# A hybrid S5 and attention layer on one core: TensorE's order fixed from the first load, the context's products one channel tile behind, k as filler work, and the modulation sums in free columns of the drives' banks

## The chip, the cores and the metric

The kernel runs on one core of a Trainium2 chip. The metric is the device time of one execution in microseconds (us); smaller is better. The core has five engines with a queue of their own each: PE (TensorE, matrix products into PSUM banks, with the loading of weights shown as PEld), DVE (VectorE), ACT (ScalarE), POOL (GpSimd), and SP (SyncE), which here only issues DMA transfers.

## What is computed

One layer over 512 latent tokens and a prefix of 256 context tokens, 1024 channels wide, all in float32. Cut to what this case is about:

```python
mod   = silu(c) @ w_mod + b_mod            # six vectors of 1024 for the latents
mod_c = silu(c_ctx) @ w_mod + b_mod        # for the context only two of them are used
sh1, sc1, g1, sh2, sc2, g2 = split(mod, 6)
h  = rmsnorm(x, norm1_w) * (1 + sc1) + sh1
hc = rmsnorm(ctx, norm1_w) * (1 + csc1) + csh1
q, k, v, u, g = split(h @ w_in)            # 1024, 256, 256, 512, 2048 columns
kc, vc, uc = split(hc @ w_in[:, Q_END:U_END])
q, k, kc = rope(rmsnorm(q)), rope(rmsnorm(k)), rmsnorm(kc)
attn  = softmax(q @ [kc, k].T / sqrt(128)) @ [vc, v]
y_ssm = s5_bidirectional(u, uc, ...)       # complex-diagonal scans, both directions
x = x + g1 * merge(attn, y_ssm, g)         # gates, glu, output projection
x = x + g2 * conv_ffn(rmsnorm(x) * (1 + sc2) + sh2)
out = rmsnorm(x) * final_norm_w
```

## The kernel before

**Tiles.** Channels lie on partitions: x is eight tiles of 128x512, ctx eight of 128x256. Every large product is made of three products of rounded parts (`mm3`, L122): hi by hi, hi by lo, lo by hi. A weight tile is loaded in pieces of 128x512 into a ring `wr` of three buffers; ACT rounds it (`wh`, L135) and POOL takes the rest (`wl`, L136). All loads are issued by SP, one after the other, each when its buffer is free.

**PSUM.** Eight banks: two of tag "a" (mod, kp, kss, vp, proj, mods), two of tag "b" (n, uc, gps, kps, yt), and two pairs of tag "s" (`bank2`; ul, then gp).

**Stages on PE, in order.** (1) The sums of squares of x (L357 and L358: eight products with ones, one for each tile's squares) and of ctx (L339, L341: added on DVE first). (2) For each channel tile k: `mod_sums(k)`, 16 rows of work on the first two modulation vectors; a copy of the sum to SBUF (L390); `mod_turn(k)`, which turns it onto partitions (L383); the scale and shift (L400, L402); h and c in two parts (L416 to L418); and the products of u, latent (`ul`) and context (`uc`), with the weight tile `wu`. (3) u is copied to SBUF, written to DRAM (`ud`) and read back in another layout (`u`, `s5_u`). (4) The keys (`kp`, their norms `kss`). (5) S5 in four blocks s of two halves h each: `s5_build` (tables W and H on DVE), `s5_lags` (kps, then the trip `ldr`, `tp` through DRAM), `s5_drive` (transposes gps, then the drive products gp), `s5_half` (products, scans and products back on DVE), `s5_out` (the readout, into the columns 384 to 511 of the drive's two banks) and `s5_end` (`yt`). (6) Attention, merging and the feed-forward network.

**What sets the order.** Up to the first drive the framework's scheduler orders all queues; from `pinned[0] = True`, just ahead of `s5_drive(0, 0)`, PE runs in program order (`pe`, L120). From there `filler()` supplies steps of v (`vp`) and gate products (`proj`), and `weave` puts them between the steps of the S5 chain. Between the filler's own steps, one step of `mods_all` (L738) is put in for every two and a half: it works out the other four modulation vectors, 16 pieces of 256 columns. Each piece is two visits of four matmuls (`mods<-wm`, L743) into a bank of tag "a" of its own, a copy of the row on ACT (L749), and a visit that turns it (`mods<-cst,vr`, L383) with two ACT operations (L755) that take the result. Its weights `wm` are 32 loads of 512 KB into two buffers.

Of the kernel before, what the change touches and what calls it, by code (L numbers as in the profile page):

```python
# [29 lines left out]
LOADS = "xxwcw"  # L30
WU_V = ()
PO2 = 2
GAP, F0, F1, F2, F3, WM = 2, 8, 13, 5, 2, 2
# [29 lines left out]
def hybrid_layer_kernel(ctx: ExitStack, tc: tile.TileContext, io, out):  # L63
    nc = tc.nc
    V, A, G, T, S = nc.vector, nc.scalar, nc.gpsimd, nc.tensor, nc.sync
# [54 lines left out]
    def pe(ins):  # L120

        if pinned[0]:  # L122
            nosync(ins, last[0])
        last[0] = ins
# [67 lines left out]
    x = [None] * 8  # L192
    cx = k8("y8", [KT, LC])
    i = 0
    for what in LOADS:
        if what == "x":
            xt = k8("x8", [4, L])
            S.dma_start(xt, io["x"][:, 4 * i:4 * i + 4])
            x[4 * i:4 * i + 4] = [xt[:, j] for j in range(4)]
            i += 1  # L200
        elif what == "c":
            S.dma_start(cx, io["ctx"])
            S.dma_start(sd, io["sd"])
        else:
            load_wm()
# [23 lines left out]
    behind = [None]  # L229

    def tt(o, a, b, op, eng=V):
        i = eng.tensor_tensor(o, a, b, op=op).ins  # L232
        if behind[0] is not None:
            nosync(i, behind[0])
# [17 lines left out]
    z1, z2, ang8 = sm("n"), sm("n2"), sm("a8")  # L252
    r1, r8 = sm("r1"), sm("r8")
    wrap(ang, r1, z1)
    V.tensor_scalar(r1, r1, PI_LO, -PI_LO, op0=OP.min, op1=OP.max)
    table("silu_and_others")
    sn, co, ab = sm("sn"), sm("co"), sm("ab")
    act(sn, r1, AF.Sin)
    A.activation(ab, r1, AF.Abs)
    act(co, ab, AF.Sin, scale=-1.0, bias=half_pi)  # L260
    V.tensor_scalar(ang8, ang, float(TC), None, op0=OP.mult)
    wrap(ang8, r8, z2)
    fr, fhi, flo = sm("fr"), sm("fhi"), sm("flo")
    V.tensor_scalar(fr, r8, 1.0 / TWO_PI, None, op0=OP.mult)
    V.tensor_scalar(fhi, fr, 192.0, None, op0=OP.add)
    V.tensor_scalar(fhi, fhi, 192.0, None, op0=OP.subtract)
    tt(flo, fr, fhi, OP.subtract)

    pw = tz([8, 2, 32], "tab", 2)
    pf = tz([8, 2, 32], "tab", 2)  # L270
    tt(pw[:, 0, 0], mag, co, OP.mult)
    tt(pw[:, 0, 1], mag, sn, OP.mult)

    def cmul(o, a, b, n):
# [41 lines left out]
    for kk, w, n in ((ka, wa, 6), (kb, wb, 16)):  # L316
        def by_s(t):
            return t.rearrange("p (s c) a -> p s (c a)", s=4)
# [127 lines left out]
    def run(gen):  # L446
        for _ in gen:
            pass
# [736 lines left out]
```

## Time and profile before

| | us |
|---|---|
| three timed executions | 983.08, 982.51, 981.89 (median 982.51) |
| the profiled execution | 982.85 |
| its span, first to last instruction | 980.8 |
| PE busy | 927.6 (95%) |
| DVE, ACT, POOL busy | 485.7, 417.0, 364.8 |

The profiled execution is 0.34 us above the median, and 2.05 us of it lie outside the span. PE is the engine that is nearly always busy. Its granted clock is shown as PEclk, 1.00 for the full 2.4 GHz and 0.5 for 1.2 GHz. A matmul's record is its own duration; how far apart two starts are says what a row of work costs PE, since they overlap. Matmuls in plain float32 (n, mod, mods, gp, kps, gps, yt) show two records for each one that the program writes, transposes one.

The rows shown further on divide the span by what PE does: to the first u product, to the last one, to the end of the first readout, to the first norm of a query (from where on attention begins), and the rest.

### The profile page before, as it was taken

To read this page: it belongs to the slowest core of one execution; us is meant where nothing else is said; L and a number is where in the kernel's file an instruction comes from. 1 tells how busy PE (TensorE), PEld (TensorE's weight loads), DVE (VectorE), ACT (ScalarE), POOL (GpSimd) and SP (SyncE) were. 2 spreads that over 40 slices of the span, in tenths; PEclk is the share of its full clock that TensorE was granted. 3 is DMA by queue.
4 is the path that set the end of the run, shared out by engine and by line. 5 is a ranking of instruction groups with operands and counts; after the bars stand their busy time and mean duration, and the time that the engine had idled before them with its cause. 6 is when DMAs were issued, how large, how long until landed. Compare 5 with 4: busy or idle time off the path is not lost.

```text
span 980.8 us, 15658 instructions
## 1 busy us (share of the span) xinstructions
PE 927.6 (95%) x6142; PEld 736.8 (75%) x6142; DVE 485.7 (50%) x935; ACT 417.0 (43%) x795; POOL 364.8 (37%) x282
## 2 busy tenths in 40 slices
PE   5998889898999999999999999999999999999996
PEld 2676766565667778888778899888888888888886
DVE  7557788484507677777524464333333333200103
ACT  7325544333228445445433443443434444432332
POOL 1214131224124122222235520555565565554553
PEclk9989999899999999999999999999999999999999
DMA  9516546464532111111114620323323233333332
GB/s 363 231 44 194 160 135 189 130 191 155 152 128 76 33 44 48 53 52 44 43 57 138 193 87 1 108 86 99 96 88 104 88 97 98 83 103 94 96 108 86
DMA packets 56378, 107.24 MB, mean 109 GB/s; under 512 B 6001, under 2 KB 19057, under 8 KB 54641
## 3 DMA queue, kind: packets, MB, share of 16 engines
q1 hardware_dynamic: 56304, 106.25, 34.4%
q8 instruction: 48, 0.79, 0.3%
q14 instruction: 26, 0.20, 0.1%
HBM read 101.02 MB, written 5.21 MB: 108 GB/s over the span
## 4 chain that ended last, share of the span: by engine, by line
PE 67%; DVE 8%; ACT 5%; issue 5%; DMA 2%; POOL 1%; DVEq 0%; ACTq 0%; POOLq 0%
PE up L127 25%; PE down L127 12%; PE proj L127 10%; PE po L127 6%; PE glu L127 3%; PE sc L127 3%; PE pab L127 3%; PE tps L906 2%; DMA wr<-wo 2%; ACT P L108 1%; ACT wh L135 1%; DVE w L232 1%; DVE p L232 1%; DVE p L587 1%; DVE k L232 1%
## 5 line engine op out<-in xcount | busy, mean ns | idle before, releaser
L136 POOL TENSOR_TENSOR wl<-wr,wh 128x512 fp32r<-128x512 f32 x226 | 312.0, 1401 | 574.7 <-ACT wh L135 565.9
L127 PE MATMUL up<-t,wh 128*128 128x512 f32 (+1 forms) x768 | 226.5, 379 | 1.3 <-DVE t L1023 0.7
L135 ACT CAST wh<-wr 128x512 fp32r<-128x512 f32 x226 | 128.1, 610 | 132.6 <-PE down L127 40.5
L127 PEld LDWEIGHTS up<-t,wh 128*128 128x128 f32 x768 | 141.1, 190 | 31.2 <-DVE t L1023 1.5
L127 PE MATMUL proj<-h,wh 128*128 128x512 f32 x384 | 145.3, 425 | 7.0 <-ACT x L108 4.0
L127 PE MATMUL up<-t,wl 128*128 128x512 f32 (+1 forms) x384 | 145.3, 378 | 0.0
L127 PEld LDWEIGHTS proj<-h,wh 128*128 128x128 f32 x384 | 74.4, 194 | 35.4 <-issue 11.7
L127 PEld LDWEIGHTS up<-t,wl 128*128 128x128 f32 x384 | 73.0, 190 | 14.5
L127 PE MATMUL proj<-h,wl 128*128 128x512 f32 x192 | 77.2, 402 | 0.8 <-POOL wl L136 0.8
L1057 DVE SCALAR_TENSOR_TENSOR zc<-up,pv,zc 128x511 f32<-128x511 f32 x44 | 33.0, 750 | 88.6 <-ACT zc L1056 88.6
L1056 ACT ACTIVATE zc<-up,pv 128x512 f32<-128x512 f32 x44 | 34.2, 778 | 74.8 <-PE up L127 74.8
L1088 DVE SCALAR_TENSOR_TENSOR x<-down,mods,x 128x512 f32<-128x512 f32 (+1 forms) x9 | 6.2, 691 | 91.5 <-PE down L127 91.5
L135 ACT CAST pth<-tps 128x512 fp32r<-128x512 f32 x48 | 28.1, 586 | 47.3 <-PE tps L906 47.3
L127 PE MATMUL glu<-w,wh 128*128 128x512 f32 x128 | 42.5, 393 | 0.0
L127 PEld LDWEIGHTS proj<-h,wl 128*128 128x128 f32 x192 | 37.5, 195 | 6.0 <-POOL wl L136 1.1
L894 DVE TENSOR_REDUCE sc<-sc 128x1 f32<-128x768 f32 x32 | 30.7, 959 | 20.1 <-PE sc L127 20.1
L136 DVE TENSOR_TENSOR ptl<-tps,pth 128x512 fp32r<-128x512 f32 x48 | 33.0, 687 | 13.3 <-ACT pth L135 13.0
L127 PE MATMUL sc<-g,qh 128*128 128x256 f32 (+1 forms) x128 | 36.8, 341 | 0.0
L127 PE MATMUL down<-h,wh 128*128 128x512 f32 x112 | 35.6, 389 | 0.0
L108 ACT ACTIVATE P<-sc,nb,rq 128x768 f32<-128x768 f32 x32 | 31.9, 996 | 5.0 <-DVE nb L895 4.0
L127 PE MATMUL po<-pth,g 128*128 128x512 f32 x96 | 33.0, 424 | 1.0 <-ACT pth L135 0.6
L1058 DVE SCALAR_TENSOR_TENSOR zc<-up,pv,zc 128x511 f32<-128x511 f32 x44 | 33.0, 750 | 1.6
(292 smaller groups left out, 1719.6 us busy)
## 6 DMA issues: line engine op xcount, KB each, us to landing
wr<-wup SPq DMA_DIRECT2D x88, 256.0 KB, 2.7
wm<-wmB SPq DMA_DIRECT2D x32, 512.0 KB, 3.7
wr<-wdn SPq DMA_DIRECT2D x40, 256.0 KB, 2.7
x<-x SPq DMA_DIRECT2D x4, 1024.0 KB, 5.2
g<-wmA SPq DMA_DIRECT2D x4, 1024.0 KB, 11.0
w<-wmA SPq DMA_DIRECT2D x4, 1024.0 KB, 12.9
wr<-wgs SPq DMA_DIRECT2D x16, 256.0 KB, 2.8
wr<-wga SPq DMA_DIRECT2D x16, 256.0 KB, 3.2
```

What stands on the lines that cost most here:

```text
L108: i = A.activation(*a, **k).ins
L127: pe(T.matmul(ps, l, r, start=start, stop=stop).ins)
L135: A.copy(hi, src)
L136: eng.tensor_tensor(lo, src, f(hi), op=OP.subtract)
L232: i = eng.tensor_tensor(o, a, b, op=op).ins
L587: V.tensor_tensor_scan(zi, rho[:, c:c + 1].to_broadcast([128, NC]), pi, 0.0, op0=OP.mult, op1=OP.add)
L894: V.tensor_reduce(mx, sv, axis=AX.X, op=OP.max)
L906: pe(T.transpose(tps[:, 128 * b:128 * b + 128], Ps[h][b][:, 128 * j:128 * j + 128], ident).ins)
L1056: A.activation(z, ps, AF.Identity, scale=cw[1], bias=pv[:, PV_CB + i:PV_CB + i + 1])
L1057: V.scalar_tensor_tensor(z[:, 1:512], ps[:, 0:511], cw[0], z[:, 1:512], op0=OP.mult, op1=OP.add)
L1058: V.scalar_tensor_tensor(z[:, 0:511], ps[:, 1:512], cw[2], z[:, 0:511], op0=OP.mult, op1=OP.add)
L1088: V.scalar_tensor_tensor(x1[i][:, c], ps[:, c], g2[:, i:i + 1], x1[i][:, c], op0=OP.mult, op1=OP.add)
```

## The change

- **PE's order** is the program's from the first instruction on (`pinned[0]` is set right after the first loads). DVE's operations pass through a class `Ordered` that fixes their order too, until the last u product; after that they must only come after that stage.
- **Loads**: x (two of 1 MiB), wm of channel tile 0, wu of tiles 0 and 1 (now one load of two pieces), wm 1, then ctx, wm 2, wu of 2 and 3, wm 3. Before, ctx was the fourth load.
- **Sums of squares**: x's squares are added on DVE too, so two products with ones instead of eight. Those of ctx come after the first u product in PE's order.
- **u**: `u_of(k, False)` makes the latent products of tile k, `u_of(k - 1, True)` the context products of the tile before. The S5's step sizes and tables, which all ran ahead of this stage, are cut into steps (`discretised`), seven of which run at the start, the others as `DISC` says between the channel tiles, along with the first two `turn`s and the first steps of `s5_build(0)`.
- **Keys** become a generator at the head of `filler()`; the norm of one key tile comes in the middle of the next one's product, its bank is of tag "b". The first drive comes after nine filler steps.
- **Drives**: `s5_drive` is split into `s5_gps` (the transposes) and `s5_gp` (the products) with nothing of the filler between them; `s5_end` of a block moves next to a drive of the next one.
- **Modulation sums**: `mods_sums` makes all 16 matmuls of a piece of 256 columns in one visit, 128 columns into each of the drive's two banks, columns 384 to 511, which the readout uses later. It is called at each drive and ahead of each readout, 16 times; ACT's copy and `mods_turn` follow. Both `wm` buffers are used by one visit, and the next two loads are issued after it. The data on the host is cut to match: each of the 32 pieces is all eight channel tiles by 128 columns.

```diff
-GAP, F0, F1, F2, F3, WM = 2, 8, 13, 5, 2, 2
+EARLY, B0, B1, F0, F1, F2, WM = 4, 9, 10, 6, 18, 5, 2
+DISC = 0, 2, 2, 2, 3, 3, 3, 3, 7
...
+    class Ordered:
+
+        last, pinned, behind = None, False, None
+
+        def __getattr__(self, op):
+            def call(*a, **k):
+                i = getattr(nc.vector, op)(*a, **k)
+                prev = self.last if self.pinned else self.behind
+                if prev is not None:
+                    nosync(i.ins, prev)
+                self.last = i.ins
+                return i
+            return call
+
+    V = Ordered()
...
+    x = []
+    for i in range(2):
+        xt = k8("x8", [4, L])
+        S.dma_start(xt, io["x"][:, 4 * i:4 * i + 4])
+        x += [xt[:, j] for j in range(4)]
+    load_wm()
+    wus = [weight(io["wu"][0], [2, 512])]
+    load_wm()
     cx = k8("y8", [KT, LC])
-    i = 0
-    for what in LOADS:
-        if what == "x":
-            xt = k8("x8", [4, L])
-            S.dma_start(xt, io["x"][:, 4 * i:4 * i + 4])
-            x[4 * i:4 * i + 4] = [xt[:, j] for j in range(4)]
-            i += 1
-        elif what == "c":
-            S.dma_start(cx, io["ctx"])
-            S.dma_start(sd, io["sd"])
-        else:
-            load_wm()
+    S.dma_start(cx, io["ctx"])
+    S.dma_start(sd, io["sd"])
+    load_wm()
+    wus.append(weight(io["wu"][1], [2, 512]))
+    load_wm()
+    pinned[0] = V.pinned = True
...
+    table("silu_and_others")
+    disc = discretised()
+    steps(disc, DISC[KT])
+    table("natural_log_exp_and_others")
+    rs_x = rstd_first(lambda k: x[k], L)
...
+        if k >= KT:
+            return
         ps = bank("mod")
         vec_mat(ps, 256, [(cz[:, j], wms[k][:, j]) for j in range(KT)])
-        row = tz([256], "bb", 2)
+        row = tz([256], "vr", 2)
         V.tensor_copy(row, ps[:, 0:256])
-        return ps, row
-
-    def mod_turn(k, ps, row):
-
+        mod[k] = ps, row
+        load_wm()
+
+    def mod_turn(k):
+
+        ps, row = mod.pop(k)
         for v in range(2):
             turned_by(ps[:, 256 + 2 * v:258 + 2 * v], row[:, 128 * v:128 * v + 128], sel)
-        finish(k, ps[:, 256:258], ps[:, 258:260])
-
-    def finish(k, sh, sc):
-        V.scalar_tensor_tensor(am[:, k], sc, sc1b[:, k:k + 1],
+        V.scalar_tensor_tensor(am[:, k], ps[:, 258:260], sc1b[:, k:k + 1],
...
-    for k in range(KT):
-        n = k
-        wh, wl = weight(io["wu"][k], [512], V if n in WU_V else G)
-        load_wm()
-        load_wm()
-        turning, sums = sums, mod_sums(k + 1) if k + 1 < KT else None
-        mod_turn(k, *turning)
...
+    def u_of(k, context):
         for s in range(4):
             sl = slice(128 * s, 128 * s + 128)
-            w = (wh[:, sl], wl[:, sl])
-            mm3(ul[s // 2][:, s % 2], w, (hh[k], hl[k]), n == 0, n == KT - 1)
-            mm3(uc[s // 2][:, 256 * (s % 2):256 * (s % 2) + 256], w, (ch[:, k], cl[:, k]),
-                n == 0 and s % 2 == 0, n == KT - 1 and s % 2 == 1)
-
-
...
+            w = tuple(t[:, k % 2, sl] for t in wus[k // 2])
+            if context:
+                mm3(uc[s // 2][:, 256 * (s % 2):256 * (s % 2) + 256], w, (ch[:, k], cl[:, k]),
+                    k == 0 and s % 2 == 0, k == KT - 1 and s % 2 == 1)
+            else:
+                mm3(ul[s // 2][:, s % 2], w, (hh[k], hl[k]), k == 0, k == KT - 1)
...
+    ul = [bank2("ul") for _ in range(2)]
+    mod_sums(0)
+    mod_turn(0)
+    scaled(x[0], rs_x, hh[0], 0, 0)
+    low(x[0], hh[0], hl[0], 0, 0)
+    mod_sums(1)
+    build = s5_build(0)
+    extra = chain(disc, turn(0), turn(1), build)
+    for k in range(KT):
+        if k + 1 < KT:
+            mod_turn(k + 1)
+            scaled(x[k + 1], rs_x, hh[k + 1], k + 1, 0)
+            if k:
+                scaled(cx[:, k], rs_c, ch[:, k], k, 1)
+            low(x[k + 1], hh[k + 1], hl[k + 1], k + 1, 0)
+        elif k:
+            scaled(cx[:, k], rs_c, ch[:, k], k, 1)
+        u_of(k, False)
+        if k == 0:
+            rs_c = rstd_first(lambda k: cx[:, k], LC)
+            uc = [bank("uc", "b") for _ in range(2)]
+
+            table("silu_and_others")
+            scaled(cx[:, 0], rs_c, ch[:, 0], 0, 1)
+        low(cx[:, k], ch[:, k], cl[:, k], k, 1)
+        steps(extra, DISC[k])
+        mod_sums(k + 2)
+        if k:
+            u_of(k - 1, True)
+        if k in (2, 4):
+            wus.append(weight(io["wu"][k // 2 + 1], [2, 512]))
+    u_of(KT - 1, True)
+    V.pinned, V.behind = False, V.last
...
-    def mods_all():
-
-        yield
-        for i in range(16):
-            ps = bank("mods")
-            for p in range(2):
-                wm = pieces[2 * i + p]
-                for j in range(4):
-                    pe(T.matmul(ps[32 * j:32 * j + 32, 0:256], cz[:, 4 * p + j], wm[:, j], start=p == 0, stop=p == 1,
-                                tile_position=(0, 32 * j)).ins)
-                mods_load()
-                if p == 0:
-                    yield
-            row = tz([256], "vr", 2)
...
+    def mods_sums(c, gp):
+
+        row = tz([2, 128], "vr", 2)
+        o = slice(4 * NC, 512)
+        for i in range(2):
+            wm = pieces[2 * c + i]
+            for j in range(KT):
+                r = 32 * (j % 4)
+                pe(T.matmul(gp[r:r + 32, i, o], cz[:, j], wm[:, j], start=j < 4, stop=j >= 4, tile_position=(0, r)).ins)
+        for _ in range(2):
+            mods_load()
+        A.copy(row, gp[:, :, o])
+        return c, gp, row
+
+    def mods_turn(c, gp, row):
+        for i in range(2):
+            turned_by(gp[:, i, 4 * NC:4 * NC + 1], row[:, i], sel[:, 0:1])
+        o = PV_BMOD + 16 + 2 * c
+        for i in range(2):
+            acts["run"].append(A.activation(mods.rearrange("p v k -> p (v k)")[:, 2 * c + i:2 * c + i + 1],
+                                            gp[:, i, 4 * NC:4 * NC + 1], AF.Identity, bias=pv[:, o + i:o + i + 1]).ins)
...
-    run(s5_drive(0, 0))
+    s5_u(0)
+
+    weave(islice(build, 6 - EARLY), fill, 6 - EARLY, B0)
+    todo = iter(range(16))
+    s5_gps(0, 0)
+    m = mods_sums(next(todo), drives[0, 0])
+    s5_gp(0, 0)
+    mods_turn(*m)
+    weave(build, fill, 6, B1)
+    run(s5_lags(0))
...
-        weave(s5_half(s, 0), chain(s5_drive(s, 1), fill), 8, 6 + F0)
+        half = s5_half(s, 0)
+        next(half)
+        s5_gps(s, 1)
+        m = mods_sums(next(todo), drives[s, 1])
+        if s:
+            s5_end(s - 1, ys_)
+        s5_gp(s, 1)
+        mods_turn(*m)
+        steps(half, 3)
+        weave(half, fill, 4, F0)
+        m = mods_sums(next(todo), drives[s, 1])
         s5_out(s, 0, ys)
+        mods_turn(*m)
         if s < 3:
             weave(chain(turn(2 * s + 2), s5_build(s + 1)), fill, 15, F1)
-            weave(chain(s5_half(s, 1), turn(2 * s + 3)), chain(s5_drive(s + 1, 0), s5_lags(s + 1), fill), 8, 9 + F2)
...
+            weave(chain(half, turn(2 * s + 3)), fill, 4, F2)
+            m = mods_sums(next(todo), drives[s + 1, 0])
+            s5_out(s, 1, ys)
+            mods_turn(*m)
```

From the first norm of a query on, PE's order is as before. Three places show the moves.

ACT's queue at the start, from the last squares on (`tg<-x`, `tg<-y`: squares of x and of ctx; `tp`, `lg`: the two reciprocal roots, the logarithm first, then the exponential; `h`, `c`: the shifted tiles). Before:

```order
L339 ACTIVATE tg<-y_81 128x256 x3
L108 ACTIVATE tp<-n_203,cc 128x512
L339 ACTIVATE tg<-y_81 128x256
L135 CAST wh<-wr 128x512
L108 ACTIVATE tp<-tp 128x512
L108 ACTIVATE lg<-n_231,cc 128x256
L108 ACTIVATE lg<-lg 128x256
L102 ACT_TABLE_LOAD
L417 ACTIVATE h_263<-x_82,shm 128x512 x2
L417 ACTIVATE c_267<-y_81,shm 128x256 x2
```

and now:

```order
L367 ACTIVATE tg<-x_83 128x512 x2
L364 ACTIVATE p<-y_99 128x256
L367 ACTIVATE tg<-y_99 128x256 x3
L349 COPY p<-cst 128x192
L123 ACTIVATE tp<-n_184,cc 128x512
L367 ACTIVATE tg<-y_99 128x256
L123 ACTIVATE tp<-tp 128x512
L150 CAST wh<-wr 128x512
L443 ACTIVATE h_216<-x_81,shm 128x512 x2
L150 CAST wh<-wr 128x512
L367 ACTIVATE tg<-y_99 128x256 x3
L123 ACTIVATE lg<-n_290,cc 128x256
```

The first h moved behind four squares of ctx and two casts, and the last three squares and the root of ctx moved behind the first two tiles of h.

DVE's queue in the u stage, one channel tile (`u`, `tab`, `bb`: the tables of the step sizes). Before:

```order
L416 SCALAR_TENSOR_TENSOR x_84<-x_84,am,tp 128x512
L416 SCALAR_TENSOR_TENSOR y_81<-y_81,am,lg 128x256
L418 SCALAR_TENSOR_TENSOR h_265<-x_82,shm,h_263 128x512
L418 SCALAR_TENSOR_TENSOR c_268<-y_81,shm,c_267 128x256
L390 COPY bb<-mod 128x256
L418 SCALAR_TENSOR_TENSOR h_266<-x_84,shm,h_264 128x512
L418 SCALAR_TENSOR_TENSOR c_268<-y_81,shm,c_267 128x256
L400 SCALAR_TENSOR_TENSOR am<-mod,sc1b,pv 128x2
L402 TENSOR_SCALAR shm<-mod,pv 128x2
L416 SCALAR_TENSOR_TENSOR x_84<-x_84,am,tp 128x512
L416 SCALAR_TENSOR_TENSOR y_81<-y_81,am,lg 128x256
```

and now:

```order
L72 SCALAR_TENSOR_TENSOR x_81<-x_81,am,tp 128x512
L72 SCALAR_TENSOR_TENSOR y_99<-y_99,am,lg 128x256
L72 SCALAR_TENSOR_TENSOR h_218<-x_81,shm,h_216 128x512
L72 SCALAR_TENSOR_TENSOR c_221<-y_99,shm,c_220 128x256
L72 TENSOR_TENSOR u<-tab,sp 128x32
L72 TENSOR_TENSOR u<-u,sp 128x32
L72 TENSOR_TENSOR u<-u 128x32
L72 TENSOR_TENSOR tab<-u 128x32
L72 TENSOR_TENSOR bb<-tab 128x224 x2
L72 TENSOR_TENSOR tab<-bb 128x7x32
L72 TENSOR_TENSOR bb<-tab 128x224 x2
L72 TENSOR_TENSOR tab<-bb 128x7x32
```

Four small operations and a complex product moved in between one tile's low parts and the copy of the row (`vr<-mod`, the counterpart of `bb<-mod`) from which the next tile is turned.

PE's queue around a block's second readout (`gp<-tp,u` and `gp<-w,tg`), the block's end (`yt`) and the next drive (`gps`, `gp<-u,gt`). Before:

```order
L611 MATMUL gp<-tp,u 64x128 x4
L617 MATMUL gp<-w_775,tg 64x128 x16
L127 MATMUL proj<-h_263,wh 128x512
L127 MATMUL proj<-h_263,wl 128x512
L127 MATMUL proj<-h_265,wh 128x512
L383 MATMUL mods<-cst,vr 32x1 x8
L127 MATMUL proj<-h_263,wh 128x512
L127 MATMUL proj<-h_263,wl 128x512
L127 MATMUL proj<-h_265,wh 128x512
L627 MATMUL yt<-cst,tg 64x64 x16
L548 MATMUL gps<-cst,k_1321 128x128 x8
L127 MATMUL proj<-h_263,wh 128x512
```

and now:

```order
L805 MATMUL gp<-wm,cz 32x128 x16
L673 MATMUL gp<-tp,u 64x128 x4
L679 MATMUL gp<-w_708,tg 64x128 x16
L417 MATMUL gp<-cst,vr 32x1 x8
L610 MATMUL gps<-cst,k_1297 128x128 x8
L805 MATMUL gp<-wm,cz 32x128 x16
L689 MATMUL yt<-cst,tg 64x64 x16
L625 MATMUL gp<-u,gt 64x96 x16
L417 MATMUL gp<-cst,vr 32x1 x8
```

The sums (now `gp<-wm,cz`) and their turns moved from between the `proj` rows to the readout and to the drive, and two of them now follow each other with only a readout, a turn and the transposes between.

## Rows read from the trace of the kernel before

**Rows 1.** Stretches: length, busy PE, PEld, DVE, ACT, POOL; PE's clock; DMA share; GB/s.
```profile
0.00:26.23 26.23, 14.37 (x116) 6.22 (x116) 20.58 (x92) 20.56 (x40) 2.63 (x15) 1.00 0.93 369
26.23:77.05 50.82, 47.48 (x362) 37.07 (x353) 28.20 (x53) 14.29 (x27) 11.57 (x8) 0.90 0.33 117
77.05:126.18 49.13, 42.00 (x394) 32.76 (x392) 37.26 (x59) 27.26 (x60) 11.57 (x8) 0.97 0.60 185
126.18:299.84 173.66, 159.74 (x1733) 108.56 (x1729) 103.81 (x179) 66.35 (x157) 50.76 (x30) 0.96 0.49 153
299.84:980.80 680.96, 664.04 (x3555) 552.15 (x3554) 295.84 (x555) 288.55 (x513) 288.22 (x222) 0.99 0.27 82
```

**Rows 2.** PE's waits up to 300 us: line, awaited engine; total, times, longest.
```profile
PE proj L127 <- ACT x L108: 4.0, 3, 2.1
...
PE mods L383 <- ACT vr L749: 2.3, 2, 2.0
```

**Rows 3.** PE in time: start, duration, operation, records; a wait in brackets.
```profile
178.38 0.39 PE L127 MATMUL proj<-h,wl 128*128 128x512 f32 x1
178.61 0.39 PE L127 MATMUL proj<-h,wh 128*128 128x512 f32 x1
181.00 0.40 PE L383 MATMUL mods<-cst,vr 128*32 128x1 f32 x16 [2.00 <-ACT vr L749]
183.13 0.79 PE L127 MATMUL proj<-h,wh 128*128 128x512 f32 x1 [1.74 <-ACT x L108]
183.72 0.63 PE L127 MATMUL proj<-h,wl 128*128 128x512 f32 x1
...
187.60 0.50 PE L127 MATMUL proj<-h,wl 128*128 128x512 f32 x1
```

**Rows 4.** PE in time: half a sum, and a turn, between proj rows.
```profile
199.92 0.40 PE L127 MATMUL proj<-h,wh 128*128 128x512 f32 x1
200.24 0.64 PE L743 MATMUL mods<-wm,cz 128*32 128x256 f32 x8
200.81 0.50 PE L127 MATMUL proj<-h,wh 128*128 128x512 f32 x1
...
202.76 0.40 PE L127 MATMUL proj<-h,wh 128*128 128x512 f32 x1
203.09 0.31 PE L383 MATMUL mods<-cst,vr 128*32 128x1 f32 x16
203.33 0.50 PE L127 MATMUL proj<-h,wh 128*128 128x512 f32 x1
```

**Rows 5.** PE in time: a drive's products, and the lags behind them.
```profile
196.67 1.54 PE L562 MATMUL gp<-u,gt 128*64 128x96 f32 x32
198.14 0.59 PE L506 MATMUL kps<-w,wpad 128*32 128x112 f32 x16
198.55 0.43 PE L506 MATMUL kps<-bb,wpad 128*32 128x16 f32 x30
```

**Rows 6.** PE in time: the start of the readout that ends at 126.18.
```profile
124.56 0.66 PE L611 MATMUL gp<-tp,u 128*64 128x128 f32 x8
```

**Rows 7.** DVE in time: complex products of the tables; a channel tile, copy to copy.
```profile
14.46 0.69 DVE L232 TENSOR_TENSOR bb<-tab 128x224 f32<-128x224 f32 x2
...
46.10 0.41 DVE L390 COPY bb<-mod 128x256 f32<-128x256 f32 x1
...
48.55 0.41 DVE L390 COPY bb<-mod 128x256 f32<-128x256 f32 x1
```

**Rows 8.** ACT in time: the table load ahead of the first h.
```profile
23.74 1.28 ACT L102 ACT_TABLE_LOAD   x1
```

**Rows 9.** SP in time: u's way through DRAM, and the loads of tp.
```profile
84.02 1.05 SPq L436 DMA_DIRECT2D ud<-g  x2
89.06 2.34 SPq L443 DMA_DIRECT2D u<-ud  x2
...
105.90 4.01 SPq L517 DMA_DIRECT2D tp<-ldr  x8
```

**Rows 10.** The tile wm from 60 to 300 us: its 32 loads.
```profile
DMA to landing us min/median/max: 3.2/3.7/9.3
```

More of the change, by code (lines that the diff above doesn't have):

```diff
@@ L2 @@
 from contextlib import ExitStack
-from itertools import chain
+from itertools import chain, islice
 import concourse.bass as bass
@@ L120, in pe @@
     def pe(ins):
-        if pinned[0]:
+        if pinned[0] and last[0] is not None:
             nosync(ins, last[0])
@@ L363, in rstd_first, with run, steps @@
         return rs
-    rs_x = rstd_first(lambda k: x[k], L, True)
-    rs_c = rstd_first(lambda k: cx[:, k], LC, False)
+    def run(gen):
+        for _ in gen:
+            pass
+    def steps(gen, n):
+        for _ in range(n):
+            next(gen, None)
+    table("silu_and_others")
[3 more added lines that the diff above has]
+    rs_x = rstd_first(lambda k: x[k], L)
     sc1b = tl([8], "sc1b")
@@ L629, in s5_end @@
         A.copy(y[:, s], yt)
-    run(s5_build(0))
-    behind[0] = None
     def proj(src, i, tag="a", eng=G):
@@ L661, in keys, with normed @@
         table("natural_log_exp_and_others")
+        ws_ = [weight(io["wk"][g], [KT, 128]) for g in range(KVH)]
+        norm = []
+        def normed(g, n, off, ps, sq):
+            ss = bank("kss", "b")[:, :n]
+            mm(ss, ones, sq[:, :n], True, True)
+            kr = t2(n)
+            if off:
+                rope(ps, 1, kr, t2())
+            else:
+                A.mul(kr, ps, pv[:, PV_QK + 1:PV_QK + 2])
+            rs = sq[:, :n]
+            rstd_of(ss, n, rs, 1.0 / HD, eps)
+            V.tensor_tensor(kr, kr, rs, op=OP.mult)
+            split(kr, kh[:, g, off:off + n], kl[:, g, off:off + n])
         for g in range(KVH):
-            w = weight(io["wk"][g], [KT, 128])
+            w = ws_[g]
             for n, off in ((LC, 0), (L, LC)):
@@ new lines, in mods_turn, with filler @@
+    def mods_turn(c, gp, row):
[5 more added lines that the diff above has]
+                                            gp[:, i, 4 * NC:4 * NC + 1], AF.Identity, bias=pv[:, o + i:o + i + 1]).ins)
+    def filler():
+        yield from keys()
+        wv_ = [weight(io["wv"][i], [4, 256]) for i in range(2)]
+        w = wv_
+        for j in range(6):
+            if j == 4:
+                w = gate_w(0)
+            yield from v_tile(j, wv_)
+        ms.extend(rows("x8", F32))
+        for i in range(8 + NGA):
+            if i == 8:
+                ga.extend(rows("c8", F32))
+            gen = gate_of((ms + ga)[i], w, "a")
+            next(gen)
+            if i + 1 < 8 + NGA:
+                w = gate_w(i + 1)
+            yield
+            yield from gen
```

388 lines of the change are left out of this document (175 added, 213 removed).

## Prediction

> **What bounds the kernel now.** I read the page first: PE is busy for 95% of the span, so only what PE waits for, runs slowly, or runs needlessly can be won. Then I cut the span where PE changes its work [rows 1]. A, up to the first u product, 26.23 us: loads at 369 GB/s and the chain behind them. B, the u products, 50.82 us: 3.3 idle and a clock of 0.90, which costs 50.82 x 0.10 = 5.1. C, to the end of the first readout, 49.13 us: 7.1 idle, clock 1.5. D, to the first norm of a query, 173.66 us: 13.9 idle, clock 173.66 x 0.04 = 6.9. E, the rest, 680.96 us at 0.99, is not touched. So A to D are 299.84 us, and 24.3 idle and 13.5 of clock in B to D are the stock from which a better order can win.
>
> Next I asked what D's idle time is. The list of waits names the taking over of `proj` by ACT and the rows of `mods` [rows 2], and the trace in time shows one such place whole [rows 3]: `proj` rows run 0.23 apart (178.38, 178.61), then the turn of a modulation sum waits 2.00 for ACT's copy of the row, and the next gate product 1.74, since v, gates and sums share two banks and ACT's copies stand late in its queue. From 183.13 the rows are 0.59 and more apart: PE has dropped from its 2.4 GHz level towards 1.2, until about 187.60. That stretch of 4.5 us costs some 2.1, half of it. So a wait of 2 us costs about 4.
>
> **The change, part by part.**
>
> *A, first loads: -1.0.* 26.23 us at 369 GB/s are 9.7 MB; without the first 2 us, in which nothing has been asked for, that is 2.6 us per MiB. ctx is now fifth in line (1.5 MiB more ahead of it), and I place its landing at 18.9. ACT's queue has four squares of ctx ahead of the logarithm that the root of x needs, so what x's earlier loads win is held up until ctx is there. The second pair of wu, whose first piece lands 1.25 MiB after ctx (22.1), is cast ahead of the first h: 22.1 + cast 0.6 + h 0.7 + low part 0.7 + the copy of the row 0.4 [rows 7] + a turn 0.3 [rows 4] + four handovers put the first u product at 25.2. Six fewer products with ones are off this path. Bounds -3 (squares free at once) to +1.
>
> *B, u products: +5.2.* PE's work is 8 tiles x 12 rows x 0.23 for the latents, 22.3, half of that for the context (half the columns), 11.2, and sums, turns and two products with ones, some 10.4: 43.9. It no longer runs out of one thing: the context lags a tile, so c is never awaited. Two new waits stand against that. First, the root of ctx now lies between the first and the second tile in DVE's fixed order: ACT casts the fourth piece of wu (it lands near 26.7, after 8.8 MiB), then three squares, two matmuls, logarithm and exponential, the table load of 1.28 [rows 8], c, its low part, and only then DVE copies the row from which tile 2 is turned. I add these to 34.3, where PE's own work ends at 30.1: 4.2. Second, the steps of the tables in DVE's queue: a tile's fixed part is 46.10 to 48.55 [rows 7] plus handovers, 3.4 of PE's 5.5 per tile, which leaves 2.1. A complex product of two pairs 0.35 long each and its sums (0.69 for two records [rows 7]) with four small operations is 3.3; the wider pieces come to 3.9 and 3.4. So tiles 2, 4 and 5 lose 1.2, 1.8 and 1.2: 4.2. The clock, after two waits of this size, I take at 3.7 instead of 5.1. 43.9 + 4.2 + 4.2 + 3.7 = 56.0. Bounds: 47 if the steps hide, 61 if ctx lands later still.
>
> *C and D, removed: 37.1.* Together 21.0 idle, 8.4 clock. The visits: half a sum costs (200.81 - 199.92) - 0.23 = 0.66, a turn (203.33 - 202.76) - 0.23 = 0.34 [rows 4]; 32 and 16 of them are 26.5. Now there are 16 visits with 32 records of 128 columns. No such row exists here. The lags have 16 records of 112 columns on tiles of the same shape in 198.55 - 198.14 = 0.41 [rows 5], so 0.82; the drive's 32 records of 96 columns take up to 1.5 [rows 5]. I take 0.82, the row of the same tile shape: 16 x (0.82 + 0.34) = 18.6, a gain of 7.9, say 7.7; with 1.5 it is a loss of 2.9. The work of k, v and gates is the same number of rows.
>
> *C and D, added: 22.6.* (a) The first drive is reached some 9 us after the last u product, before it was 34. Then ud went out 7.0 after that product and u followed 5.0 later [rows 9]; with some 4 for landing, u is there no sooner than 13 after it, and ACT's and DVE's copies of u stand ahead. PE waits about 5.0. Before, the keys hid this. (b) The third sum needs a load of wm that SP issues behind the eight of tp, 4.01 [rows 9]: 2.4. (c) Both wm buffers are emptied by one visit, and the next two loads are issued after it. A load lands after 3.2 at best, 3.7 in the middle, 9.3 at worst [rows 10]. Where a sum ahead of a second readout is followed by the next drive's, only the readout (124.56 [rows 6] to 126.18, 1.6), a turn and the transposes, some 3.0, lie between; this happens three times, and once 2.0. At 3.7 + 0.4 for the second issue that is 3 x 1.1 + 2.1 = 5.4, and I add 2.6 for one slow landing at the others, where some 7 us of filler lie between: 8.0. (d) The first key's norm, 0.7. (e) The slow clock after such waits: half a dozen, some of them over 2 us, at up to 2.1 each as in [rows 3]; 6.5.
>
> Net of C and D: -14.5, with bounds from -29 (no waits) to +10 (slow landings).
>
> *Sum.* -1.0 + 5.2 - 14.5 = -10.3 on 982.85, the profiled execution, is 972.5; that execution stands 0.34 above the median, so 972.2 by the timed runs.
>
> **A rule to weigh.** The modulation row is now read by ACT from the same bank that PE fills with the drive and that DVE then reads; before, it had its own bank. The trace of before shows nothing of three engines on one bank. The Trainium skill, "PSUM — Partial Sum Buffer", section Terms, says that two engines on the same bank and quadrant at once are an error, reads against reads included. By that rule DVE, ACT and PE have to be kept apart there. It is the third rival below; no row here prices it.
>
> **The rivals.**
>
> 1. *The new waits don't come.* u is there in time, wm lands at its best 3.2, and the front is no longer than before. For it: in [rows 10] half of the loads land within 3.7, and the fewer ring loads of the start leave SP freer. Against it: u's way through DRAM is in the rows [rows 9] and nothing shortens it. With B at its old length, (c) at 2.0 and (e) at 2.0: 972.2 - 5.2 - 6.0 - 4.5 = 956.5.
> 2. *Slower: wm is late.* SP issues in order, and a load that must wait for its buffer holds back all behind it, the ring of weights and tp among them; two loads of 512 KB at once also share the engines with them. At the worst landing of [rows 10], 9.3, the four tight places cost 3 x 6.7 + 7.7 = 27.8 and six of the others 2.7 each, 44 in all against the 8.0 taken: 1008. It decides from a mean landing near 6.5, where the four places cost 17 and no gain but a few us is left. For it: before, a load had a whole half visit's time more. Against it: the middle is 3.7 with the same queue.
> 3. *No change: the shared banks serialise.* DVE can't start on a drive until ACT has taken the modulation results, and each drive's chain grows by the copy, the turn and the take-off, 1.1 each, in eight halves: 8.8, so 981. Filler products should hide it, so I give it little.
>
> **How the numbers follow.** 0.2% (2 us) is about what a measurement of this kernel can tell from no change. The forecast, 964 to 979: 58%. Rival 1, 952 to 963: 18%. Rival 3 with 980 to 984: 10%. Rival 2, 985 to 1008: 14%, of which a little lies within 0.2%. So faster 0.77, within 0.2% 0.10, slower 0.13. The range from 955 to 988 leaves out about half of rival 2 and the tails of rival 1 and of the bounds in B.
>
> **What would show it.** In the profile after: the first u product near 25, a wait of some 4 us ahead of the second tile's turn, the last u product near 81 instead of 77; a wait for u ahead of the first drive products; no wait of `proj` for ACT; waits for wm in the tight places, at most 4 us each; the first norm of a query near 289 instead of 299.84, and E at 681. A front that ends before 77 makes rival 1 likely; sums that wait over 6 us make it rival 2.

## The result: slower by 2.7%

| | median, us | span of the profiled execution |
|---|---|---|
| before | 982.8 (981.89 to 985.1) | 980.8 |
| after | 1009.34 (1008.07 to 1013.23) | 1007.0 |

The ratio is 1.0273, with a 95% interval of 1.0240 to 1.0306: 26.5 us slower, where 10 us faster was forecast. The time lies outside the range of 955 to 988, and 1.3 beyond the worst end of the second rival (985 to 1008), to which the prediction gave 14%. The median of before is that of four executions; the fourth, beside the three of the first table, took 985.1.

The stretches of the kernel after, cut at the same events as [rows 1] (first u product 28.10, last one 85.72, end of the first readout 132.42, first norm of a query 322.40), in the same columns:

```profile
0.00:28.10 28.10, 5.92 (x68) 2.36 (x69) 17.15 (x55) 16.28 (x32) 5.63 (x17) 1.00 0.94 366
28.10:85.72 57.62, 48.27 (x399) 35.50 (x390) 42.14 (x94) 24.04 (x43) 10.65 (x7) 0.94 0.31 105
85.72:132.42 46.70, 36.04 (x417) 27.93 (x416) 40.29 (x54) 22.35 (x48) 8.70 (x6) 0.89 0.66 199
132.42:322.40 189.98, 162.72 (x1966) 132.68 (x1962) 112.95 (x189) 72.97 (x169) 46.46 (x30) 0.91 0.44 135
322.40:1007.00 684.60, 666.07 (x3555) 551.41 (x3554) 295.25 (x552) 283.95 (x506) 287.34 (x222) 0.99 0.28 82
```

| stretch | before | forecast | after | off by |
|---|---|---|---|---|
| A | 26.2 | 25.2 | 28.1 | +2.9 |
| B | 50.8 | 56.0 | 57.6 | +1.6 |
| C and D | 222.8 | 208.3 | 236.7 | +28.4 |
| E | 681.0 | 681.0 | 684.6 | +3.6 |

So the mistake lies in C and D, where the gain was to be. PE is idle there for 10.66 + 27.26 = 37.9 us (21.0 before, 16.1 forecast), and its clock costs 46.70 x 0.11 + 189.98 x 0.09 = 22.2 (8.4 before, 6.5 forecast). The two overlap, since a stretch's clock is a mean over its idle time too. PE's waits up to 340 us (line, awaited engine: total, times, longest) say for what, and are to be held against [rows 2]:

```profile
PE n L142 <- DVE sc1b L72: 18.5, 1, 18.5
PE gp L805 <- DMA wm<-wmB: 13.7, 8, 4.7
PE mod L417 <- DVE vr L72: 10.3, 6, 3.1
PE kps L586 <- ACT gt L612: 7.7, 2, 4.4
PE gp L625 <- ACT vr L808: 3.7, 4, 1.7
PE gps L610 <- DVE k L72: 3.6, 1, 3.6
PE kp L142 <- DVE tg L72: 3.1, 1, 3.1
PE proj L142 <- ACT wh L150: 2.5, 1, 2.5
PE n L142 <- DVE p L72: 2.0, 1, 2.0
```

`proj`'s three waits for `x` and the 2.0 of the turn, on which the change was argued, are gone. In their place stand three kinds of waits that the change brings: for a load of `wm` (13.7), for ACT around a drive (`kps`, 7.7; the row of the sum in the drive's bank, 3.7), and for DVE in the part whose order is now fixed (`mod`, the first `gps`, `n`). The list doesn't say which of them decides; the experiments take them away one by one and together.

### The profile page after: what moved, and what is told of

Same layout as the page of the kernel before. It is cut to its first block, busy times and chain, and to the rows that moved or that the text cites. A ratio compares the mean times of both kernels' runs of the same rounds, so it can differ in the third digit from the quotient of the medians.

```text
span 1007.0 us, 16139 instructions
## 1 busy us (share of the span) xinstructions
PE 919.0 (91%) x6386; PEld 749.9 (74%) x6386; DVE 507.8 (50%) x941; ACT 419.6 (42%) x796; POOL 358.8 (36%) x282
## 4 chain that ended last, share of the span: by engine, by line
PE 72%; DVE 12%; DMA 6%; ACT 5%; issue 3%; POOL 1%; DVEq 0%; ACTq 0%; POOLq 0%
PE up L142 24%; PE down L142 12%; PE proj L142 10%; PE po L142 5%; PE sc L142 3%; DVE p L72 3%; PE glu L142 3%; PE pab L142 3%; DMA wm<-wmB 2%; DVE t L72 2%; PE tps L993 2%; PE gp L625 2%; DMA wr<-wo 2%; PE vp L142 2%; ACT wh L150 1%
## 5 line engine op out<-in xcount | busy, mean ns | idle before, releaser
L151 POOL TENSOR_TENSOR wl<-wr,wh 128x512 fp32r<-128x512 f32 x226 | 306.7, 1378 | 604.0 <-ACT wh L150 597.0
L142 PE MATMUL proj<-h,wh 128*128 128x512 f32 x384 | 133.9, 416 | 2.5 <-ACT wh L150 2.5
L805 PE MATMUL gp<-wm,cz 128*32 128x128 f32 x512 | 20.9, 303 | 13.8 <-DMA wm<-wmB 13.7
```

The lines of the kernel that those rows point to most:

```text
L142: pe(T.matmul(ps, l, r, start=start, stop=stop).ins)
L151: eng.tensor_tensor(lo, src, f(hi), op=OP.subtract)
L805: pe(T.matmul(gp[r:r + 32, i, o], cz[:, j], wm[:, j], start=j < 4, stop=j >= 4, tile_position=(0, r)).ins)
```

## Experiments

Each ratio stands against runs of the kernel before on the same chip (medians 983.1 for experiments 1 to 4, 984.7 for 5 to 8, 984.9 for 9 to 11, 983.5 for 12). The kernel after was not run again beside them, so a difference in us between two of these groups, or against the kernel after, is uncertain by some 2 us, as much as these medians lie apart; there the ratios are the better measure. Diffs are against the kernel after.

**1. No late loads.** The first two loads of `wm` are used for all sums, 30 loads and with them the right weights are left out.

```diff
-            wm = pieces[2 * c + i]
+            wm = pieces[i]
...
-        for _ in range(2):
-            mods_load()
```

> The changed kernel, but 30 of the 32 loads of wm are left out: every sum uses the first two pieces, so the modulation vectors are computed from the wrong weights. All else stays. In the profile of the changed kernel the sums wait 13.7 us for wm on PE. Theory W (late wm loads, through the waits and the slow clock behind them, are most of what the stretch after the u products lost): 22 to 30 us faster than the changed kernel, so 980 to 987, and no wait for wm. Theory Q (late copies on ACT and late tables on DVE take the place of any single wait that is removed): 13.7 at most and rather 8, so 996 to 1002.

999.63 us, ratio 1.0169 (1.0148 to 1.0190). The waits for `wm` are gone and only 9.7 us with them. The list of PE's waits from 85 to 320 us now begins with one that stood nowhere in the kernel after:

```profile
PE gp L679 <- DVE tg L72: 7.1, 4, 2.7
PE kps L586 <- ACT gt L612: 4.0, 1, 4.0
```

The readout (L679) waits for DVE's products; in the kernel after, as I read it, the late loads held PE up ahead of it for longer. Taken away alone, with all the rest as it is, the late loads give back 9.7 of the 26.5 us.

**2. The front left to the scheduler.** PE's and DVE's orders are free until the last u product; everything behind it is as in the kernel after.

```diff
-    pinned[0] = V.pinned = True
...
     fill = filler()
+    pinned[0] = True
```

> The changed kernel, but PE's and DVE's order is left to the scheduler up to the last u product, as before the change; PE's order is fixed only from the first drive's filler on. The source order of that stage stays. Theory F (the fixed order itself makes the front longer, 85.67 us to the last u product instead of 77.05): the last u product comes at 76 to 79, the whole at about 1001. Theory of the lag and the moved tables (the length comes from what DVE has to do between two channel tiles, whoever orders it): the last u product stays at 84 or later, the whole at 1007 to 1011.

992.08 us, 1.0088 (1.0059 to 1.0117). The stretches:

```profile
0.00:23.00 23.00, 6.01 (x68) 2.54 (x68) 17.96 (x79) 16.71 (x34) 4.22 (x16) 0.98 0.92 360
23.00:77.92 54.92, 47.94 (x389) 35.68 (x390) 49.66 (x81) 23.28 (x46) 11.74 (x8) 0.94 0.45 165
77.92:114.92 37.00, 32.32 (x418) 25.46 (x416) 24.59 (x44) 20.35 (x45) 8.06 (x6) 1.00 0.73 220
114.92:304.70 189.78, 162.91 (x1964) 132.59 (x1960) 115.88 (x189) 74.04 (x170) 46.95 (x30) 0.91 0.43 136
```

A is shorter by 5.1, B by 2.7, C by 9.7; D is as long as in the kernel after (189.78 against 189.98), and E 1.4 longer. The largest part is won in C, whose order this edit doesn't touch: DVE is busy for 49.66 in B instead of 42.14 and for 24.59 in C instead of 40.29. Left alone, it builds the first tables while PE makes u; in the fixed order that work is still to do when the first drive comes. The wait of 3.6 for DVE's `k` is gone. But the largest wait for ACT in D is as before, to the tenth:

```profile
PE kps L585 <- ACT gt L611: 7.7, 2, 4.4
```

So this wait does not come from the front.

**3. Turns behind the transposes' copy.** ACT's first step of a later `turn` is put behind the copy of `gt`, for which `kps` waited.

```diff
         i = A.activation(wq, wv, AF.Identity, bias=magic)
+        if lastgt[0] is not None:
+            nosync(i.ins, lastgt[0])
...
-            A.copy(gt, gps...)
+            lastgt[0] = A.copy(gt, gps...).ins
```

The place it is about, in the kernel after, rows of DVE, ACT and PE in time:

```profile
186.02 4.53 DVE L72 TENSOR_TENSOR w<-w,t 128x1024 f32<-128x1024 f32 x2
...
193.10 0.61 ACT L466 ACTIVATE t<-t,cc 128x384 f32<-128x384 f32 x1 [7.10 <-DVE t L72]
193.62 1.05 ACT L612 COPY gt<-gps 128x512 f32<-128x512 f32 x2
...
194.24 0.59 PE L586 MATMUL kps<-w,wpad 128*32 128x112 f32 x16 [3.26 <-ACT gt L612]
```

The instruction ahead of the copy of `gt` in ACT's queue waits 7.10 for a step of DVE's tables, and the copy starts only behind it.

> The changed kernel, but on ACT the first step of each turn of the scan angles comes only after the copies of the transposes gps that the program makes before it. In the profile of the changed kernel PE waits 7.7 us at kps for the bank that these copies free, and ACT stands 6 to 7 us at a turn whose DVE input is late. Theory Q (the queue of ACT is what holds the drives): the wait at kps goes from 7.7 to under 2, and with the clock 8 to 12 us go, so 997 to 1001. Theory W: the wait moves to the next wm load, no more than 3 us go, 1006 to 1009.

1007.76 us, 1.0262 (1.0227 to 1.0298): 1.6 us won, within the error. `kps` no longer waits; the drive's own products do, behind the other copy that stands behind the turn, that of the sum's row:

```profile
195.70 0.61 ACT L467 ACTIVATE t<-t,cc 128x384 f32<-128x384 f32 x1 [2.92 <-DVE t L72]
196.22 0.35 ACT L811 COPY vr<-gp 128x256 f32<-128x256 f32 x1
196.62 1.65 PE L628 MATMUL gp<-u,gt 128*64 128x96 f32 x32 [2.34 <-ACT vr L811]
```

These products write other columns of the bank than the row lies in, and still start only when ACT has read it. Such waits for `vr` are 7.9 in this kernel, 3.7 in the one after.

**4. The sums back in banks of their own**, as before, with everything else as after (`mods_all` with `wm` pieces of 256 columns, between the filler's steps).

> The changed kernel with the modulation sums put back as they were before: half visits of four matmuls between filler steps, in a bank of tag a of their own, wm in the former layout, one load issued after each half visit; they start behind the keys. Everything else of the change stays. Theory W: the waits for wm go, those of the shared banks (13.9 us of idle time before) come back in part, about 15 us faster than the changed kernel, 990 to 998. Theory Q, with little from the loads: the visits cost 8 more and the waits come back, 1010 to 1020.

1005.1 us, 1.0218 (1.0196 to 1.0240). The shared bank is gone from this kernel, and of PE's waits for `wm` one of 2.6 is left; it is only 4.2 us better. New waits stand in their place, the largest one again for ACT's copy of a transposed tile:

```profile
PE yt L689 <- ACT gt L612: 5.9, 3, 3.3
```

So with the front fixed, moving the sums back wins little. That doesn't price the pairs of sums: the old place has a price of its own (32 half visits and 16 turns are 26.5 us of PE by [rows 4]), and experiment 9 spreads the sums with the front fixed and comes to 1.0095.

**5. PE's order fixed, DVE's free.**

```diff
-    pinned[0] = V.pinned = True
+    pinned[0] = True
```

> The changed kernel with PE's order fixed from the first load as in the change, but DVE's order up to the last u product left to the scheduler. Leaving both to it gave 992.1, 17 less than the changed kernel. Theory D (it is DVE's fixed order that costs: the adding of x's squares, the row copies behind the steps of the tables, the late first tables of the drive): most of the 17 is had, 993 to 997, the last u product at 78 to 81. Theory P (PE's fixed order costs: one tile's late turn holds all products): 1003 to 1009, the last u product at 83 or later.

998.89 us, 1.0143 (1.0101 to 1.0184), somewhat nearer to experiment 2 than to the kernel after. A is 23.4 and C 39.8, nearly as in experiment 2; B is 60.4, the longest but one of all kernels. `mod`'s turn still waits for DVE's copy of the row:

```profile
PE mod L417 <- DVE vr L72: 8.7, 7, 2.5
```

So A and C suffer from DVE's fixed order, and B from PE's: when the copy is late, PE may take nothing else first.

**6 and 7. The front free, and the sums spread.** Experiment 6 is experiment 2 with one change: of the two sums next to each other at a drive (each into a pair of banks of its own), one moves into the middle of the filler work between two drives. The last block has no such stretch behind it; there the sum goes into the middle of the half. Experiment 7 also puts later turns behind both copies: to experiment 3's edit comes the row's.

```diff
-        m = mods_sums(next(todo), drives[s, 1])
...
-            weave(chain(turn(2 * s + 2), s5_build(s + 1)), fill, 15, F1)
+            gen = chain(turn(2 * s + 2), s5_build(s + 1))
+            weave(islice(gen, 7), fill, 7, 9)
+            drives[s + 1, 0] = bank2("gp")
+            m = mods_sums(next(todo), drives[s + 1, 0])
+            weave(islice(gen, 2), fill, 2, 2)
+            mods_turn(*m)
+            weave(gen, fill, 6, F1 - 11)
...
-        A.copy(row, gp[:, :, o])
+        lastgt[0] = A.copy(row, gp[:, :, o]).ins
```

Why the pair costs, in the kernel after, PE in time behind a readout:

```profile
157.26 0.31 PE L417 MATMUL gp<-cst,vr 128*32 128x1 f32 x16
157.50 1.09 PE L610 MATMUL gps<-cst,k 128*128 128x128 f32 x8
159.02 0.65 PE L805 MATMUL gp<-wm,cz 128*32 128x128 f32 x16 [0.43 <-DMA wm<-wmB]
162.79 1.08 PE L805 MATMUL gp<-wm,cz 128*32 128x128 f32 x16 [3.13 <-DMA wm<-wmB]
```

A visit needs two loads. The first is 0.43 late, the second 3.13 more. Both are issued at 155.33, right behind the visit that empties the buffers, and SP goes on with the loads of `tp`:

```profile
155.33 0.80 SPq L794 DMA_DIRECT2D wm<-wmB  x2
...
156.71 7.62 SPq L597 DMA_DIRECT2D tp<-ldr  x8
```

> Front left to the scheduler (992.1 as such), and the modulation sums spread: the sum that followed a second readout, 3 us after the former one, is made in the middle of the filler between two halves instead, and the last one seven filler steps later, so that some 8 us or more lie between any two. Theory W2 (what wm costs is the short distance between two sums): the waits for wm go from 11.7 us to under 4, and with the clock 8 to 12 go, 980 to 984. Rival (the loads are late because SP issues them behind other loads): waits of 7 or more stay, 988 or more.

> As the run with the free front and the spread sums, and on ACT the first step of each turn of the scan angles comes after the copies of the transposes and of the modulation row that stand before it in the program. The run with only the former half of this bought nothing, since the drive's products then waited for the row's copy, in whose bank they write, and that stood behind the turn. Theory Q2 (both copies have to be ahead): the waits at kps and gp, 9.5 us with the free front, go under 4, 5 to 9 us less than without it, 973 to 978. Rival (DVE's tables are late anyway and the wait moves to the next readout): 0 to 2 less.

Experiment 6: 977.25 us, 0.9925 (0.9900 to 0.9949). Experiment 7: **971.79 us**, 0.9866 (0.9840 to 0.9893), faster than the kernel before and than the one after. D falls from experiment 2's 189.78 to 176.38 and 169.08. The waits for `wm` fall from 11.7 us in experiment 2 to 1.1 and to none, though a load lands hardly sooner (in the middle 4.9, 4.8 and 4.7 in experiments 2, 6 and 7): what helps is the distance between the visits. The stretches C and D of experiment 7, and two of the waits that are left in them:

```profile
77.82:114.22 36.40, 32.86 (x418) 25.99 (x417) 23.73 (x42) 20.17 (x44) 7.91 (x6) 0.99 0.77 232
114.22:283.30 169.08, 156.05 (x1966) 126.45 (x1962) 116.93 (x189) 73.04 (x169) 43.66 (x30) 0.96 0.50 150
```
```profile
PE gp L682 <- DVE tg L72: 6.7, 2, 3.6
...
PE kps L588 <- DVE w L72: 1.7, 2, 1.2
```

Idle is 3.5 + 13.0 = 16.6 and clock 0.4 + 6.8 = 7.1: about the 16.1 and 6.5 that the prediction had put into its sum. They are other waits than it named: 6.7 is the readout waiting for DVE's products, and none is for `u` or `wm`.

**8. The front free, the sums back** (the edits of 2 and 4).

> Front left to the scheduler, and the modulation sums put back into half visits in a bank of their own: what remains of the change is the lag of the context's products, the moved tables, the keys as filler and the early drive. From the sum of the two single runs (17 and 4 less than the changed kernel): 988. If the remainder were a gain by itself, as forecast for the removed waits, it would come under 982.

992.35 us, 1.0081 (1.0053 to 1.0109), as experiment 2 (992.08). With a free front, too, the sums as the change places them buy nothing over their old place; spread, they buy 15.1 (experiment 6), and with the later turns 20.6 (experiment 7).

**9 and 10. The other way round.** Experiment 9 has the spread sums and late turns of experiment 7 with the front fixed as in the change; experiment 10 has the late turns alone.

> The changed kernel with its fixed front kept, and both later remedies: the sums spread, and on ACT the turns behind the copies of transposes and rows. If the costs add up (front 17, sums 15, turns 5): 971.8 + 17 = 989, the last u product at 85 to 87 as in the changed kernel, and from there to the first norm of a query 205 to 212. If the costs only show when several come together: under 980 or over 996.

> The changed kernel with only this edit: on ACT the turns come behind the copies of transposes and of rows. The former try held them behind the transposes alone and bought 1 to 2 us, with 7.9 us of waits at gp. Theory Q2 (the drive's products need the row's copy, since they write in its bank): the waits at kps and gp fall from 11.4 to under 5, 4 to 8 us faster than the changed kernel, 1001 to 1005. Rival (the wait moves to wm): 1007 to 1009.

Experiment 9: 994.35 us, 1.0095 (1.0057 to 1.0133), 22.6 above experiment 7; 13.0 of the profile's difference lie in C, 9.5 in A and B. Experiment 10: 1014.21 us, 1.0303 (1.0254 to 1.0352); its interval overlaps with that of the change, so nothing is won. There `kps` no longer waits for ACT's copy but for the tables:

```profile
PE kps L589 <- DVE w L72: 10.2, 6, 3.4
```

My reading is that a turn that starts later makes the tables later, which the next drive needs. What was a remedy of 5.5 us between experiments 6 and 7 wins nothing where two sums still stand side by side and the front is fixed.

**11. The filler shared out anew** on experiment 7 (8, 16 and 6 steps in place of 6, 18 and 5).

> The fastest so far (free front, spread sums, turns behind the copies; 971.8) with two more filler steps ahead of each first readout, one more ahead of each second one, and two fewer between them. In its profile two first or second readouts wait 6.7 us in all for DVE's half. If these waits are what is left: under 2 us of them, 4 to 7 us faster with the clock, 965 to 968. If the filler is then missing between the halves, where DVE builds the tables: waits at kps instead, 971 to 976.

970.41 us, 0.9850 (0.9807 to 0.9893), the best time of all, but not to be told from experiment 7.

**12. The row's copy first.** In DVE's fixed order the copy for which `mod` waits is put ahead of the table steps.

```diff
-        steps(extra, DISC[k])
         mod_sums(k + 2)
+        steps(extra, DISC[k])
```

> The changed kernel, all of its order kept, but in the u stage the steps of the tables come behind the copy of the next but one tile's row in DVE's queue instead of ahead of it (two lines of the program swapped). Theory D (PE's turns wait for that copy because the table steps stand ahead of it, 10.3 us in six waits, the last u product at 85.7): the waits of mod for DVE fall under 5, the last u product comes at 80 to 83, the whole 3 to 6 lower, 1003 to 1006. Rival (DVE has too much to do in each tile, and where it stands makes no difference): ul waits for h instead, the last u product stays at 85 or later, 1007 to 1012.

1014.0 us, 1.0312 (1.0277 to 1.0347). `mod` waits nearly as long (9.3 instead of 10.3), the wait at `uc` grows from 0.7 to 2.8, and the last u product starts at 88.9 instead of 85.6. So moving the copy within a tile doesn't help. In B of the kernel after, DVE is busy for 42.14 of 57.62 us and PE for 48.27. My reading, which this run supports and doesn't prove, is that with both so full, wherever the copy stands something that PE needs stands behind it, and PE may not go round it.

## Why the prediction was wrong

The step that failed is the sum for C and D, and in it two terms. "Removed" took all 21.0 us of old waits as gone and "added" put four new ones in their place, 16.1; 37.9 came, of which 17.5 are for late results of DVE, ACT and POOL and had no term, and 5.3 are loads sized too small. And the clock, put at 6.5 on half a dozen waits, took 22.2. The front added 4.5 to that.

**The front (A).** The landing of ctx was right: ACT starts on it at 18.94, where 18.9 was said. That it decides was wrong. DVE's adds of x's squares, which are new, decide:

```profile
11.94 6.42 DVE L72 TENSOR_TENSOR p<-p,tg 128x512 f32<-128x512 f32 x6
...
18.50 2.04 PE L142 MATMUL n<-p,ones 128*128 128x512 f32 x2 [18.50 <-DVE sc1b L72]
```

ACT's last square ends near 16.0, and the adds run to 18.3, since they stand behind table steps and two of the six run beside POOL (last section); then the turn of the row waits 3.13 for its copy. With a free order the same product with ones starts 4.3 us sooner:

```profile
14.20 1.73 PE L142 MATMUL n<-p,ones 128*128 128x512 f32 x2
```

The prediction counted six fewer products on PE and gave DVE's adds no term: of a step that moves to another engine it followed only the engine that it left.

**The u products (B).** Right. Two waits of 4.2 each were forecast. The first, for the root of ctx, is 2.0 (`n` for the squares of ctx) and 1.8 (`mod` for `vr`); the second, for the table steps, is 0.6, 3.0 and 1.2 (`mod` for `vr`). With 0.7 at the end that is 9.4 of idle, and the clock costs 57.62 x 0.06 = 3.5 where 3.7 was taken.

**The first drive (a).** 5.0 was forecast for u. The wait is 3.6 for DVE's `k`, 0.7 for its copy and 1.7 for the sum's row, 6.0, and u is there in time. The size was right by luck, the cause wrong: the tables of the first block were taken as done. (The 13 us allowed for u's way are also less than the sum of the terms given for it, 7.0, 5.0 and 4.)

**(b) and (d).** The third sum waits 0.4 instead of 2.4, the key's norm 0.7 as said.

**The loads (c).** 8.0 forecast; of the 13.7 measured 0.4 belong to (b), so 13.3. The four places are those named, the landing isn't: the tile's loads between 60 and 330 us land later in the middle than in [rows 10].

```profile
DMA to landing us min/median/max: 3.5/5.0/7.7
```

With 5.0 for 3.7 the four places would cost 5.4 + 4 x 1.3 = 10.6; they cost 13.3, because a visit waits for the second of its two loads. The 2.6 for the other places were not needed. The second rival had asked for a mean landing near 6.5, or for 44 us of waits at 9.3; the middle is 5.0 and the waits 13.3, and still its time came, from other causes.

**What had no term.** All waits of PE in C and D come to 37.9. 16.1 had been forecast; 5.3 more are (c), 1.0 more (a), 2.0 less (b). The other 17.5 are `kps` (7.7), `kp` for its norm's scaling on DVE (3.1), the weights at `proj` (2.5 and 0.9), and 3.3 more for ACT at the drives. Most of this is a chain through three queues: DVE's tables are late, ACT's turn stands ahead of the copies and waits for them, and PE waits for the copies. The lateness behind `kps` isn't inherited from the front, since experiment 2 has the same 7.7 with the front free; a part of it is that table steps run beside POOL (last section). The prediction looked at each queue by itself, and the third rival's "filler products should hide it" is the sentence that fell: between transposes, sum and products there is no filler left, by the change's own design. The rule weighed there, that engines are to be kept apart in a bank (the Trainium skill, "PSUM — Partial Sum Buffer", section Terms), tells of errors, and no run here shows one. What the rows show at that place is a wait: in experiment 3 the drive's products are held until ACT has read the row. That wait costs 5.0 in the kernel after (3.7 and 0.8 for `vr`, 0.5 for `mods`), against the 8.8 in the third rival.

**The clock (e).** The largest mis-sized term: 6.5 was said for C and D, 22.2 measured. Half a dozen waits were counted; the list has 22 in C and D. With the waits mended, in experiment 7, the same stretches have 0.99 and 0.96.

**What held.** A visit of a sum was to cost 0.82; in the kernel after, its start and that of the next operation lie 148.04 - 147.15 = 0.89 apart:

```profile
147.15 1.08 PE L805 MATMUL gp<-wm,cz 128*32 128x128 f32 x32
148.04 0.57 PE L586 MATMUL kps<-w,wpad 128*32 128x112 f32 x16
```

Where the idle time and the clock come to about the forecast sums, as in experiment 7 (by luck, since the waits are others), so does the rest: C and D take 205.5 there (208.3 forecast), and PE's own work, length less idle and clock, falls from 193.4 to 181.8, by 11.6 where 7.7 was said.

So the account of the 26.5 us by experiments: the fixed front costs 17.3 (experiment 2 against the kernel after) to 22.6 (7 against 9); the pairs of sums 14.8 (2 against 6); the turns ahead of the copies 5.5 (6 against 7). These are three steps of one way from the kernel after to experiment 7, so their sum, 17.3 + 14.8 + 5.5 = 37.6, is the whole difference by construction. 26.5 of it is the loss, and 11 the gain over the kernel before that is left when all three are mended (12.9 against its runs on the same chip), close to the 10 that were forecast. The prices hold in this order only, as 3, 4, 10 and 12 show: taken singly, each mended wait shows the next one.

**Open.** E is 684 to 688 in all kernels with the sums in the drives' banks, 681 before (in experiments 4 and 8 it is 692 and 694, with 22 gate products more behind the first norm of a query). The 3.6 arise in the middle of E, where neither code nor order was changed; a wait of 1.9 at 591.91, `po` for DVE's `x`, is new there, and no run separates their cause. Why the fixed front costs 22.6 with the other faults mended and 17.3 with them wasn't tried; that some of it is hidden behind the late loads is only likely. Whether the context's lag of a tile gains anything by itself wasn't tried either.

## What to carry to other kernels

An order fixed by hand is worth what its worst-covered wait allows: before fixing one engine's order, write down for every engine that feeds it what stands ahead of the awaited instruction, and leave to the scheduler the parts where several engines are close to full. Two users of a double buffer belong as far apart as the landing time of both loads, and here a bank shared by columns made ACT's read of it a wait for PE. When a wait is taken away and the time barely moves, read the list of waits again before judging the idea: here the same idea was 2.7% slower or 1.3% faster, by the spacing of the sums, the order of two copies and the front.

## What the runs showed of the hardware

DVE's sums of two tiles in SBUF slow down when POOL works at the same time. Of the six adds of 128x512 in A of the kernel after, three start before POOL's two subtractions, two beside them, and one behind (rows of DVE and POOL in time, the adds singly):

```profile
11.94 0.68 DVE L72 TENSOR_TENSOR p<-p,tg 128x512 f32<-128x512 f32 x1
...
14.31 1.57 DVE L72 TENSOR_TENSOR p<-p,tg 128x512 f32<-128x512 f32 x1
15.99 1.57 DVE L72 TENSOR_TENSOR p<-p,tg 128x512 f32<-128x512 f32 x1
17.66 0.69 DVE L72 TENSOR_TENSOR p<-p,tg 128x512 f32<-128x512 f32 x1
```
```profile
14.01 3.01 POOL L151 TENSOR_TENSOR wl<-wr,wh 128x512 fp32r<-128x512 f32 x2 [12.12 <-ACT wh L150]
```

That is 0.69 against 1.57, a factor of 2.3, and it is why six adds last 6.42 in A. At 186.02 two sums of 128x1024 take 2.30 each, where the same operation has a mean of 1.21 in experiments 7 and 10, while POOL has two subtractions that take 3.90 (a row of POOL in time):

```profile
185.56 3.90 POOL L151 TENSOR_TENSOR wl<-wr,wh 128x512 fp32r<-128x512 f32 x2 [1.49 <-ACT wh L150]
```

The Trainium skill, "SBUF — State Buffer", section Who interferes with whom, says that a DVE instruction with two SBUF inputs contends with a GpSimd instruction that reads SBUF. The trace agrees, with these numbers; whether one is held for a whole instruction of the other or they take turns, its rows don't show.

The second thing is how much a wait costs beyond itself: from the kernel before to the one after, PE's idle time in C and D rises by 16.9, and the loss to the clock, reckoned over the whole stretch, by 13.8.
